# Hybrid encoder layer on one core: last gate multiplied into blocks on chip, sums held one product ahead, residuals and scale rows loaded in the middle of products

## The chip, the core and the metric

The kernel runs on one core of a Trainium2 chip. TensorE (PE) multiplies matrices, VectorE (DVE), ScalarE (ACT) and GpSimd (POOL) do elementwise work, SyncE (SP) issues most DMAs, and GpSimd issues some. The metric is device time in microseconds; the kernel before took 2562.34 us (median of three runs, 2558.35 to 2562.83).

## The reference

The layer normalises 1280 tokens of width 2048 (a prompt of 1024 and a sample of 256), projects them, runs neighbourhood attention on one half of the columns and a bidirectional mLSTM on the other, gates both, and projects the mixed rows back onto the residual:

```python
    hn = rmsnorm(x, norm_w)
    proj = jnp.einsum('btd,dp->btp', hn, w_in)
    ...
    att = (att * jax.nn.silu(na_g)).astype(x.dtype)
    ...
    h = rmsnorm(h, head_norm_w.reshape(ML_HEADS, ML_HEAD_DIM)).reshape(B, T, ML_WIDTH)
    mem = (h * jax.nn.sigmoid(ml_o.astype(f32)) * jax.nn.silu(ml_z.astype(f32))).astype(x.dtype)
    mixed = jnp.concatenate([att, mem], axis=-1)
    return x + jnp.einsum('btm,md->btd', mixed, w_out)
```

A last RMSNorm with the weights `final_norm_w` follows. Everything is in float32. The kernel reaches that precision by splitting each operand in a high and a low part (`split`: ScalarE casts the high part, VectorE subtracts it from the source for the low part) and adding three products of the parts.

## The kernel before

The end of the program is what the change touches. Tokens stand in two groups: the first 768 (`GA`) and the last 512 (`GB`). The gates of the mLSTM for the last 512 tokens are projected late, in four calls of `late_gate` (`LATE` = 0, 2, 4, 6), each for two blocks `k` of 128 mixed columns. Each call computes the gate in `z_`, loads the ungated columns of the mixed rows `mixT[k]` from DRAM into `th`, multiplies, and stores them back. The last call is for `k` = 14 and 15.

Then comes the output projection. The mixed rows are loaded by GpSimd's queue as blocks of 128 columns and 640 tokens, `mb<kh><th><kk>`: `kh` is the half of the columns, `th` the half of the tokens, `kk` one of eight blocks; `mb116` and `mb117` hold the columns 14 and 15 for the last 640 tokens. In the code the four sets are `Aa` (0,0), `Ae` (0,1), `Ad` (1,0) and `Ac` (1,1). The projection is done by a scheme of seven products in place of eight on 2 x 2 halves, once for each half `p` of the output columns, so 14 products `product(p, i, ...)`, in the order 2, 5, 1, 6, 7, 4, 3 for `p` = 0 and 5, 1, 6, 7, 4, 3, 2 for `p` = 1. Each product has eight blocks `kk`; a block is three matmuls for each of five token tiles. `operands(p, i, kk)` gives a block's two operands, which are often sums made by VectorE: of mixed blocks (`ms`, or in place in `mb01x`), of weights (`T2`, `wb`). Both operands are split (`mo` for the mixed rows, `wo` for the weights; 4 buffers each). Blocks 6 and 7 of a product (`HOLD`) are multiplied tile by tile at its end, and `reads` then adds each tile into the residual tiles `y`; `y_done` squares a finished tile (`jk`), scales it by a row of final weights (`fnb`) and stores it for `p` = 0.

Weights come on SyncE's queue in three ways: single blocks `wb` and `T` of 256 KB (six buffers `po` for `wb`), and pairs of blocks of 512 KB, which go in turn either to the two buffers that the input projection uses too (`wr_wp`) or to one tile of their own (`wp`, every third pair). Residuals are loaded into slots that the normalised inputs leave (`xslot`): for `p` = 0 on GpSimd's queue, for `p` = 1 on SyncE's.

The order of the instructions on each engine is set by a scheduler that takes from the traced program what it deems ready first; a queue is then worked off strictly in that order. `tc.issue_after(ins)` only sets such an order: what is traced inside it stands behind `ins` on the engine of `ins`, without a wait for its end.

Of the kernel before, what the change touches and what calls it, by code (L numbers as in the profile page):

```python
# [13 lines left out]
P = 128  # L14
# [31 lines left out]
def kernel(  # L46
# [23 lines left out]
    def f(ap):  # L70
        return ap.bitcast(F32)
# [91 lines left out]
    def split(hi, lo, src, scale=None):  # L163
        if scale is None:
            S.copy(hi, src)  # L165
            V.tensor_tensor(lo, src, f(hi), op=ALU.subtract)  # L166
        else:
            S.mul(hi, src, scale)
            V.scalar_tensor_tensor(lo, src, scale, f(hi), op0=ALU.mult, op1=ALU.subtract)

    def split_a(hi, lo, src):
        S.copy(hi, src)
# [520 lines left out]
        return out  # L693

    def late_gate(ch, X):
        os_ = proj_pair(OT0 + ch, X, True)
        for o_ in os_:
            S.activation(o_, o_, AF.Tanh, scale=0.5)
        for j, z_ in enumerate(proj_pair(ZT0 + ch, X, True)):
            k = 8 + ch + j  # L700
            th = po(f"lt{k}")[:, :GB]
            S.activation(th, z_, AF.Tanh, scale=0.5)
            V.scalar_tensor_tensor(z_, th, 1.0, z_, op0=ALU.add, op1=ALU.mult)
            V.scalar_tensor_tensor(z_, os_[j], 1.0, z_, op0=ALU.add, op1=ALU.mult)
            DM.dma_start(th, mixT[k][:, GA:])
            V.scalar_tensor_tensor(z_, th, w4_sb[:, k - 8 : k - 7], z_, op0=ALU.mult, op1=ALU.mult)
            DM.dma_start(mixT[k][:, GA:], z_)

    def proj_v(u, X):
        gates = u == NA_H // 2  # L710
# [764 lines left out]
        [u for us in na for u in us],  # L1475
    )
    for ch in LATE:
        late_gate(ch, X)
    att_ctx.close()

    mp = ctx.enter_context(tc.tile_pool(name="mp", bufs=1))
# [13 lines left out]
    Ad = [mix_block(1, 0, kk) for kk in range(8)]  # L1495
    Ae = [mix_block(0, 1, kk) for kk in range(8)]
    Ac = [mix_block(1, 1, kk) for kk in range(8)]
    Aa = [mix_block(0, 0, kk) for kk in range(8)]
    fnb = [xslot(28 + i, f"fnb{i}") for i in range(4)]
    T2 = {}  # L1500
    Y = {}
    ss = [mp.tile([P, 4], F32, tag=f"oss{t}", name=f"oss{t}") for t in range(2 * NT)]

    pair_of = {}

    def w_block(kh, nb, kk, name):
        raw = po(f"wb_{name}")[:, :512]
        DM.dma_start(raw, w_o[nb, :, (8 * kh + kk) * 512 : (8 * kh + kk + 1) * 512])
        return raw

    def w_pure(kh, nb, kk, name):
        k = 8 * kh + kk
        if kk % 2 == 0:
            src = w_o[nb, :, k * 512 : (k + 2) * 512]
            pair_of["n"] = pair_of.get("n", -1) + 1
            if pair_of["n"] % 3 == 2:
                pair_of["w"] = mp.tile([P, 1024], F32, tag="wr2", name=f"wp_{name}")
                DM.dma_start(pair_of["w"], src)
# [45 lines left out]
    def y_init(p, q):  # L1564
        th, nh = divmod(q, 2)
        for tt in range(NT):
            y_ = Y[p, q, tt] = xslot(q * NT + tt, f"y{p}_{q}_{tt}")
            r0 = (th * NT + tt) * P
            q_ = DM if p else G
            q_.dma_start(y_, xtok[r0 : r0 + P, (2 * p + nh) * 512 : (2 * p + nh + 1) * 512])  # L1570

    def y_done(p, q, tt):
# [9 lines left out]
    def finish(th, tt):  # L1582
# [13 lines left out]
        for i in (2, 0, 3, 1):  # L1596
# [5 lines left out]
                V.tensor_scalar(out[i], out[i], rs, None, op0=ALU.mult)  # L1602
            DM.dma_start(y[t * P : (t + 1) * P, i * 512 : (i + 1) * 512], out[i])

    HOLD = 2

    def product(p, i, bk, first, each):
        held = []
        tail = (p, i) == (1, 2)

        def mms(tt, kk, m, w, last):
# [6 lines left out]

        for kk in range(8):
            nm = f"{p}_{i}_{kk}"  # L1620
            ms, wsrc = operands(p, i, kk)
            if tail:
                m = [
                    mp.tile([P, TH], F32R, tag=f"mb{z}{z}{kk}", name=f"mo{nm}_{z}") for z in range(2)
                ]
            else:
                t = mp.tile([P, 2, TH], F32R, tag="mo", name=f"mo{nm}", bufs=4)
                m = [t[:, z] for z in range(2)]
            split(*m, ms)
            if tail and kk >= 4:  # L1630
                w = [xslot(2 * kk + 12 + z, f"wt{nm}_{z}", F32R) for z in range(2)]
            else:
                t = wb.tile([P, 2, 544], F32R, tag="wsp", name=f"wo_{nm}", bufs=4)
                w = [t[:, z, :512] for z in range(2)]
            split(*w, wsrc)
            if tail or kk >= 8 - HOLD:
                held.append((kk, m, w))
                continue
            for tt in range(NT):
                mms(tt, kk, m, w, False)  # L1640
        for tt in range(NT):
            for kk, m, w in held:
                mms(tt, kk, m, w, kk == 7)
# [4 lines left out]
    def p_banks(p, j):  # L1648
        return [bank("pr" if next(slots) == "p" else "a", f"po{p}_{j}_{i}") for i in range(NT)]

    for i in range(4):
        DM.dma_start(fnb[i], fnw[i * 512 : (i + 1) * 512].partition_broadcast(P))
    SUB = ALU.subtract
    for p in range(2):

# [124 lines left out]
```

## Time and profile before

| | |
|---|---|
| median of three runs | 2562.34 us (2558.35 to 2562.83) |
| the profiled execution | 2565.18 us, span 2563.3 us |
| TensorE busy | 2534.0 us, 99% of the span |
| VectorE, ScalarE, GpSimd busy | 77%, 52%, 24% |
| output projection, first to last matmul | 2160.00 to 2553.89 us |
| after the last matmul | last tiles added, squared, scaled and stored |
| DMA | 503.03 MB, mean 196 GB/s |

The page calls TensorE busy 99% of the span, but the ends of its matmuls are modelled, so the count of matmuls in a stretch tells more than the share. All times of the trace count from the start of the span. In its rows a name such as `wr_wp<-in_w_o_dram` is the written tile and what it is read from, with buffer numbers left out; a bracket tells how long the engine was idle just before and what ended that. `SPq` and `POOLq` are the queues on which DMAs are issued.

### The profile page before, as it was taken

Reading aid. Unit: us, or ns where it says so; the run is one execution under the profiler, and the core shown is the slowest. Engines: PE = TensorE matmul, PEld = TensorE weight load, DVE = VectorE, ACT = ScalarE, POOL = GpSimd, SP = SyncE. Lnnn points to the kernel's source line nnn. Section 1 sums busy time; section 2 is a strip of 40 time slices with the busy share of each in tenths; the row PEclk is TensorE's granted clock in tenths of the full one; section 3 lists DMA queues with packets and bytes.
Section 4 is the critical chain, followed back from the end, with each engine's and each line's share of the span. In section 5 each row is a group of like instructions: output and inputs, shape, how many; then the busy total and the mean of one; then the engine's idle time right before and its main releaser. Section 6 shows DMA issues by size and latency. Waiting matters only on the chain.

```text
span 2563.3 us, 44540 instructions
## 1 busy us (share of the span) xinstructions
PE 2534.0 (99%) x15054; PEld 2368.6 (92%) x15054; DVE 1972.6 (77%) x4029; ACT 1345.0 (52%) x3041; POOL 615.3 (24%) x909
## 2 busy tenths in 40 slices
PE   8999999999999999999999999999999999999998
PEld 8999999999999999999999999998988887788886
DVE  8769888888869798898875866765855665879695
ACT  8535545444444444465655666655745543344444
POOL 0535555444544444410001110100100104000001
PEclk9999999999999999999999999999999999999999
DMA  6546464536434342467768878877867849636237
GB/s 215 174 143 200 143 199 130 179 124 200 125 112 126 101 141 89 154 228 223 239 223 299 297 243 272 293 234 261 286 197 251 277 126 377 202 125 218 85 87 254
DMA packets 303483, 503.03 MB, mean 196 GB/s; under 512 B 48752, under 2 KB 191256, under 8 KB 303256
## 3 DMA queue, kind: packets, MB, share of 16 engines
q1 hardware_dynamic: 299096, 484.46, 58.9%
q0 software_dynamic: 4160, 15.73, 1.6%
q8 instruction: 119, 1.95, 0.3%
q14 instruction: 108, 0.88, 0.1%
HBM read 373.13 MB, written 126.95 MB: 195 GB/s over the span
## 4 chain that ended last, share of the span: by engine, by line
PE 92%; DMA 5%; DVE 2%; issue 1%; ACT 1%; SPq 0%; POOL 0%; ACTq 0%; POOLq 0%; DVEq 0%
PE pc L662 16%; PE po L1613 14%; PE pv L740 5%; PE fb L274 2%; PE A24b L274 1%; PE A12b L274 1%; PE A16b L274 1%; PE A44b L274 1%; PE A48b L274 1%; PE A52b L274 1%; PE A40b L274 1%; PE A20b L274 1%; PE A8b L274 1%; PE A50b L274 1%; PE A42b L274 1%; PE A22b L274 1%
## 5 line engine op out<-in xcount | busy, mean ns | idle before, releaser
L1613 PE MATMUL po<-wo,mo 128*128 128x512 f32 x1620 | 376.9, 393 | 3.7 <-ACT wo L165 2.8
L1613 PEld LDWEIGHTS po<-wo,mo 128*128 128x128 f32 x1620 | 303.6, 188 | 76.2 <-ACT wo L165 4.2
L166 DVE TENSOR_TENSOR ws<-wr,ws 128x512 fp32r<-128x512 f32 x152 | 104.3, 696 | 53.2 <-ACT ws L165 52.4
L165 ACT CAST ws<-wr 128x512 fp32r<-128x512 f32 x152 | 92.5, 617 | 70.1 <-PE pc L662 57.5
L165 ACT CAST mo<-mb 128x640 fp32r<-128x640 f32 x72 | 51.8, 726 | 92.5 <-PE po L1613 73.7
L116 POOL TENSOR_SCALAR rs<-rs 128x1 f32<-128x1 f32 x10 | 3.4, 341 | 351.2 <-DVE rs L1593 351.1
L166 DVE TENSOR_TENSOR mo<-mb,mo 128x640 fp32r<-128x640 f32 x72 | 59.1, 827 | 27.1 <-ACT mo L165 27.0
L1562 DVE TENSOR_TENSOR y<-y,po 128x512 f32<-128x512 f32 x90 | 58.5, 687 | 11.3 <-PE po L1613 11.0
L165 ACT CAST mo<-ms 128x640 fp32r<-128x640 f32 x40 | 28.9, 726 | 61.1 <-PE po L1613 32.1
L166 DVE TENSOR_TENSOR wsv<-wr_v,wsv 128x512 fp32r<-128x512 f32 x64 | 44.4, 700 | 14.2 <-ACT wsv L165 13.9
L165 ACT CAST wsv<-wr_v 128x512 fp32r<-128x512 f32 x64 | 39.0, 617 | 26.8 <-PE pv L740 15.5
L1576 ACT ACTIVATE jk<-y 128x512 f32<-128x512 f32 x40 | 25.2, 631 | 36.5 <-DVE y L1562 36.2
L413 DVE SCALAR_TENSOR_TENSOR pcv<-pco,cw_sb,pcv 128x516 f32<-128x516 f32 x48 | 36.7, 764 | 7.1 <-ACT pcv L407 7.0
L166 DVE TENSOR_TENSOR mo<-ms,mo 128x640 fp32r<-128x640 f32 x40 | 32.8, 823 | 7.6 <-ACT mo L165 7.6
L129 ACT ACTIVATE xq<-xq 128x1024 f32<-128x1024 f32 x20 | 21.2, 1061 | 31.7 <-DMA xq<-in_xtok_dram 29.2
L1081 POOL MEMSET mls_0v<- 128x2 f32 x4 | 0.4, 102 | 145.1 <-DVE S_dt.float L166 119.7
L274 PE MATMUL fb<-xg,fw 128*128 128x384 f32 x192 | 34.6, 334 | 0.0
L251 DVE TENSOR_TENSOR pco<-pc,rstdb 128x512 f32<-128x512 f32 x30 | 20.6, 687 | 17.8 <-PE pc L662 17.1
L274 PEld LDWEIGHTS fb<-xg,fw 128*128 128x128 f32 x192 | 33.4, 188 | 0.0
L778 DVE CUSTOM_DVE_ANT_0 nap_0st<-nap_0s,nap_0bt 128x384 f32<-128x384 f32 x32 | 17.7, 555 | 20.1 <-PE nap_0s L773 8.7
L1525 DVE TENSOR_TENSOR ms<-mb,mb 128x640 f32<-128x640 f32 x40 | 32.8, 823 | 0.0
L1492 POOL DMA_DIRECT2D mb<-mx x32 | 17.7, 554 | 58.8 <-DVE ws L166 24.8
(2655 smaller groups left out, 8512.4 us busy)
## 6 DMA issues: line engine op xcount, KB each, us to landing
wr<-in_w_in_dram SPq DMA_DIRECT2D x76, 512.0 KB, 4.7
wr_v<-in_w_in_dram SPq DMA_DIRECT2D x32, 512.0 KB, 5.0
wb<-in_w_o_dram SPq DMA_DIRECT2D x48, 256.0 KB, 3.0
xq<-in_xtok_dram SPq DMA_DIRECT2D x20, 512.0 KB, 4.2
mb<-mx POOLq DMA_DIRECT2D x32, 320.0 KB, 8.2
wr_wp<-in_w_o_dram SPq DMA_DIRECT2D x16, 512.0 KB, 4.0
vS<-vo SPq DMA_DIRECT2D x24, 256.0 KB, 5.1
nap_0bt<-in_rpb_tab_dram SPq DMA_DIRECT2D x32, 192.0 KB, 4.3
```

The source lines that it names most:

```text
L129: S.activation(raw, raw, AF.Square, accum_out=ssq[g][:, t, q : q + 1])
L165: S.copy(hi, src)
L166: V.tensor_tensor(lo, src, f(hi), op=ALU.subtract)
L251: V.tensor_tensor(o, src, rb, op=ALU.mult)
L274: PE.matmul(o, w(a_), x(b_), start=first and m == 0, stop=last and m == 2)
L413: V.scalar_tensor_tensor(dst[:, a:n], src[:, a + j - pad : n + j - pad], cw_sb[:, ct, j : j + 1], dst[:, a:n], op0=ALU.mult, op1=ALU.add,)
L662: PE.matmul(pb[j], t[j][:, wi, c : c + P], xs[xi], start=first and m == 0, stop=last and m == 2,)
L740: PE.matmul(outs[tt], xs[:, tt * P : (tt + 1) * P], t[:, wi, q * w : (q + 1) * w], start=first and m == 0 and (gates or tt % 2 == 0), stop ...
L1525: V.tensor_tensor(t, x, y_, op=op)
L1562: V.tensor_tensor(Y[p, q, tt], Y[p, q, tt], bk, op=op)
L1576: S.activation(jk, Y[p, q, tt], AF.Square, accum_out=ss[t][:, c : c + 1])
L1613: PE.matmul(bk[tt], m[xi][:, tt * P : (tt + 1) * P], w[wi], start=first and kk == 0 and j == 0, stop=last and j == 2, skip_group_check=True,)
```

## The change

There are three parts. First, the last call of `late_gate` no longer loads, multiplies and stores `mixT`: it returns its two gates, and they are multiplied into the loaded blocks `Ac[6]` and `Ac[7]` (`mb116`, `mb117`), with the same factor `w4_sb`. Second, the operands of a block are traced behind the split of the same block in the product before (`done`, filled from `now`), so that VectorE takes up a product's sums one product ahead and not sooner. Third, the residual tiles of `p` = 0 other than the first set go on SyncE's queue, and they and the scale rows are issued in the middle of products: `product` takes `loads` and the block `when` at which they are issued, behind the last `wb` load. Also every third pair of weights that goes to the tile of its own is now the first of three and no longer the last.

```diff
     def late_gate(ch, X):
+        held = []
...
             V.scalar_tensor_tensor(z_, os_[j], 1.0, z_, op0=ALU.add, op1=ALU.mult)
+            held.append(z_)
+            if ch == LATE[-1]:
+                continue
             DM.dma_start(th, mixT[k][:, GA:])
             V.scalar_tensor_tensor(z_, th, w4_sb[:, k - 8 : k - 7], z_, op0=ALU.mult, op1=ALU.mult)
             DM.dma_start(mixT[k][:, GA:], z_)
+        return held
...
     for ch in LATE:
-        late_gate(ch, X)
+        last_gates = late_gate(ch, X)
...
     Ac = [mix_block(1, 1, kk) for kk in range(8)]
+    for j, z_ in enumerate(last_gates):
+        k = LATE[-1] + j
+        t = Ac[k][:, GA - TH :]
+        V.scalar_tensor_tensor(t, t, w4_sb[:, k : k + 1], z_, op0=ALU.mult, op1=ALU.mult)
     Aa = [mix_block(0, 0, kk) for kk in range(8)]
...
     def w_block(kh, nb, kk, name):
         raw = po(f"wb_{name}")[:, :512]
-        DM.dma_start(raw, w_o[nb, :, (8 * kh + kk) * 512 : (8 * kh + kk + 1) * 512])
+        last_load["ins"] = DM.dma_start(
+            raw, w_o[nb, :, (8 * kh + kk) * 512 : (8 * kh + kk + 1) * 512]
+        ).ins
         return raw
...
-            if pair_of["n"] % 3 == 2:
+            if pair_of["n"] % 3 == 0:
...
-            q_ = DM if p else G
+            q_ = DM if p or q else G
...
+    def scales(p):
+        for i in range(4 if p == 0 else 0):
+            DM.dma_start(fnb[i], fnw[i * 512 : (i + 1) * 512].partition_broadcast(P))
+
     HOLD = 2
+    done = []
 
-    def product(p, i, bk, first, each):
+    def product(p, i, bk, first, each, loads=None, when=0):
         held = []
+        now = []
...
         for kk in range(8):
             nm = f"{p}_{i}_{kk}"
-            ms, wsrc = operands(p, i, kk)
+            if loads is not None and kk == when:
+                with tc.issue_after(last_load["ins"]) if kk else ExitStack():
+                    loads()
+            with tc.issue_after(done[kk]) if done else ExitStack():
+                ms, wsrc = operands(p, i, kk)
...
-            split(*w, wsrc)
+            now.append(split(*w, wsrc).ins)
...
+        done[:] = now
...
-    for i in range(4):
-        DM.dma_start(fnb[i], fnw[i * 512 : (i + 1) * 512].partition_broadcast(P))
...
-        y_init(p, 1)
-        y_init(p, 3)
         bk = p_banks(p, 1)
-        product(p, 5, bk, True, reads(bk, (1, ALU.add), (3, ALU.add)))
+        product(
+            p, 5, bk, True, reads(bk, (1, ALU.add), (3, ALU.add)),
+            lambda: (y_init(p, 1), y_init(p, 3)), 0 if p else 5,
+        )
...
-        product(p, 1, ch, True, reads(ch, (0, ALU.add), done=0 if p == 0 else None))
-        y_init(p, 2)
+        product(
+            p, 1, ch, True, reads(ch, (0, ALU.add), done=0 if p == 0 else None),
+            lambda: (scales(p), y_init(p, 2)), 3,
+        )
```

What the scheduler makes of it shows at three places. On SyncE's queue around the start of the output projection, before (`wr_wp_0_2_2` is the pair of weight blocks 2 and 3 of product 2, `T2` and `wb_0_5` the weights of product 5, `lt` the mixed rows for the last gate, `mx` their store):

```order
L633 DMA wr_wp_0_2_2_26553<-in_w_o_dram 128x1024
L1537 DMA T2_0_5_6_26879<-in_w_o_dram 128x512
L1537 DMA T2_0_5_7_26891<-in_w_o_dram 128x512
L1652 DMA fnb0_26476<-in_fnw_dram 128x512
L1652 DMA fnb1_26477<-in_fnw_dram 128x512
L1652 DMA fnb2_26478<-in_fnw_dram 128x512
L1652 DMA fnb3_26479<-in_fnw_dram 128x512
L633 DMA wr_wp_0_2_6_26641<-in_w_o_dram 128x1024
L705 DMA lt14_26384<-mx14_149 128x512
L1508 DMA wb_0_5_0_26715<-in_w_o_dram 128x512
L705 DMA lt15_26391<-mx15_150 128x512
L1508 DMA wb_0_5_1_26742<-in_w_o_dram 128x512
```

The same place of that queue now:

```order
L633 DMA wr_wp_0_2_4_26589<-in_w_o_dram 128x1024
L1548 DMA T2_0_5_6_26871<-in_w_o_dram 128x512
L1548 DMA T2_0_5_7_26883<-in_w_o_dram 128x512
L1529 DMA wp_0_2_6_26633<-in_w_o_dram 128x1024
L633 DMA wr_wp_0_1_0_26941<-in_w_o_dram 128x1024
L1517 DMA wb_0_5_0_26687<-in_w_o_dram 128x512
L1517 DMA wb_0_5_1_26714<-in_w_o_dram 128x512
L1517 DMA wb_0_5_2_26741<-in_w_o_dram 128x512
L1517 DMA wb_0_5_3_26768<-in_w_o_dram 128x512
L1517 DMA wb_0_5_4_26795<-in_w_o_dram 128x512
L1581 DMA y0_1_0_26822<-in_xtok_dram 128x512
L1581 DMA y0_1_1_26824<-in_xtok_dram 128x512
```

The scale rows and the loads for the last gate are gone from here, each pair of product 2's weights stands one place sooner, and ten residual tiles (the two shown and eight more) stand behind the fifth `wb`. Pair 0, which stood where pair 2 now stands (ahead of the eight `T2`), has moved to the place of the tile of its own, ahead of the last input projection's weights.

On GpSimd's queue, the end of its loads before (`y0_2_3` is a residual tile, `mb116` and `mb117` the mixed blocks of the last gate):

```order
L1570 DMA y0_2_3_27177<-in_xtok_dram 128x512
L1570 DMA y0_2_4_27179<-in_xtok_dram 128x512
L1570 DMA y0_3_0_26700<-in_xtok_dram 128x512
L1492 DMA mb116_26456<-mx14_149 128x640
L1492 DMA mb117_26458<-mx15_150 128x640
L116 TENSOR_SCALAR rs5_29151<-rs5_29151 128x1
```

And the end of its loads now:

```order
L1497 DMA mb007_26470<-mx7_142 128x640
L1581 DMA y0_0_0_26486<-in_xtok_dram 128x512
L1581 DMA y0_0_1_26488<-in_xtok_dram 128x512
L1581 DMA y0_0_2_26490<-in_xtok_dram 128x512
L1581 DMA y0_0_3_26492<-in_xtok_dram 128x512
L1581 DMA y0_0_4_26494<-in_xtok_dram 128x512
L116 TENSOR_SCALAR rs5_29147<-rs5_29147 128x1
```

Of the 20 residual loads five are left, and `mb116` and `mb117` now stand behind `mb113`, 10 loads ahead of the first residual.

On VectorE, the splits of product 1's first blocks before (`mo_0_1`, `wo_0_1`), with the first sums for product 7 (`wb_0_7`):

```order
L166 TENSOR_TENSOR wo_0_1_0_26954<-wr_wp_0_1_0_26949,wo_0_1_0_26954 128x512
L1545 TENSOR_TENSOR T2_0_5_7_26891<-wb_0_1_7_27107,T2_0_5_7_26891 128x512
L1553 TENSOR_TENSOR wb_0_7_0a_27362<-wb_0_7_0a_27362,wb_0_7_0b_27364 128x512
L166 TENSOR_TENSOR mo0_1_1_26975<-mb001_26462,mo0_1_1_26975 128x640
L166 TENSOR_TENSOR wo_0_1_1_26978<-wr_wp_0_1_0_26949,wo_0_1_1_26978 128x512
L1549 TENSOR_TENSOR mb017_26442<-mb017_26442,mb007_26474 128x640
L1553 TENSOR_TENSOR wb_0_7_1a_27390<-wb_0_7_1a_27390,wb_0_7_1b_27392 128x512
```

Where these sums stand now, among the splits of product 6 (`mo0_6`, `wo_0_6`):

```order
L166 TENSOR_TENSOR wo_0_6_0_27181<-T2_0_5_0_26689,wo_0_6_0_27181 128x512
L1564 TENSOR_TENSOR wb_0_7_0a_27358<-wb_0_7_0a_27358,wb_0_7_0b_27360 128x512
L1536 TENSOR_TENSOR ms0_7_0_27363<-mb110_26438,mb010_26422 128x640
L166 TENSOR_TENSOR mo0_6_1_27200<-mb011_26424,mo0_6_1_27200 128x640
L1573 TENSOR_TENSOR y0_0_0_26486<-y0_0_0_26486,po0_2_0_26933 128x512
L166 TENSOR_TENSOR wo_0_6_1_27203<-T2_0_5_1_26716,wo_0_6_1_27203 128x512
L1564 TENSOR_TENSOR wb_0_7_1a_27386<-wb_0_7_1a_27386,wb_0_7_1b_27388 128x512
```

The sums for product 7 have moved from product 1's splits, two products ahead, to product 6's, one ahead.

More of the change, by code (lines that the diff above doesn't have):

```diff
@@ L165, in split @@
             S.copy(hi, src)
-            V.tensor_tensor(lo, src, f(hi), op=ALU.subtract)
+            return V.tensor_tensor(lo, src, f(hi), op=ALU.subtract)
         else:
             S.mul(hi, src, scale)
-            V.scalar_tensor_tensor(lo, src, scale, f(hi), op0=ALU.mult, op1=ALU.subtract)
+            return V.scalar_tensor_tensor(lo, src, scale, f(hi), op0=ALU.mult, op1=ALU.subtract)
     def split_a(hi, lo, src):
@@ L1502 @@
     ss = [mp.tile([P, 4], F32, tag=f"oss{t}", name=f"oss{t}") for t in range(2 * NT)]
-    pair_of = {}
+    pair_of, last_load = {}, {}
     def w_block(kh, nb, kk, name):
         raw = po(f"wb_{name}")[:, :512]
-        DM.dma_start(raw, w_o[nb, :, (8 * kh + kk) * 512 : (8 * kh + kk + 1) * 512])
+        last_load["ins"] = DM.dma_start(
+            raw, w_o[nb, :, (8 * kh + kk) * 512 : (8 * kh + kk + 1) * 512]
+        ).ins
         return raw
```

## The prediction, on record before the changed kernel ran

> **What bounds the kernel now.** First the page's table of engines and its costliest group, then the stages that the change touches.
>
> ```profile
> PE 2534.0 (99%) x15054; PEld 2368.6 (92%) x15054; DVE 1972.6 (77%) x4029; ACT 1345.0 (52%) x3041; POOL 615.3 (24%) x909
> L1613 PE MATMUL po<-wo,mo 128*128 128x512 f32 x1620 | 376.9, 393 | 3.7 <-ACT wo L165 2.8
> ```
>
> TensorE is the bound, and in the output projection (L1613) it is idle for only 3.7 us. So the change can win no more than what TensorE loses there. The next view gives TensorE's matmuls in order of time: start, length, what, how many, and the wait in brackets; the last row is the end of the projection. The one after it counts the projection's matmuls in a stretch without waits.
>
> ```profile
> 2160.00 7.10 PE L1613 MATMUL po<-wo,mo 128*128 128x512 f32 x30
> 2168.93 15.68 PE L1613 MATMUL po<-wo,mo 128*128 128x512 f32 x65 [1.83 <-ACT wo L165]
> 2185.08 12.99 PE L1613 MATMUL po<-wo,mo 128*128 128x512 f32 x55 [0.47 <-DVE wo L166]
> 2199.01 1.65 PE L1613 MATMUL po<-wo,mo 128*128 128x512 f32 x6 [0.94 <-ACT wo L165]
> 2201.03 39.26 PE L1613 MATMUL po<-wo,mo 128*128 128x512 f32 x169 [0.37 <-DVE wo L166]
> ...
> 2550.95 2.94 PE L1613 MATMUL po<-wt,mo 128*128 128x512 f32 x12
> ```
>
> ```profile
> 2210.00:2530.00 320.00, 320.00 (x1385) 259.55 (x1384) 51.77 (x80) 1.00 0.48 151
> ```
>
> The projection has 14 products of 8 blocks of 15 matmuls: 1680 (1620 with `wo`, 60 with `wt`). The stretch of 320 us holds 1384 (one of the 1385 only reaches into it): 0.2312 us each, 3.47 us a block, 27.7 us a product. 1680 of them make 388.4 us, and 0.2 for the last one's longer end; the projection takes 2553.89 - 2160.00 = 393.9. So it loses 5.3 us, all before 2201: 3.61 in the four waits, the rest in starting up again after each. That is the whole prize.
>
> Why it waits: the queues. Of SyncE's queue, in order of issue (start, length, what); then ScalarE's casts of the weights, with their waits; then the DMA queues between 2116 and 2176 us.
>
> ```profile
> 2117.40 0.33 SPq L1518 DMA_DIRECT2D wp<-in_w_o_dram  x1
> 2144.86 0.33 SPq L633 DMA_DIRECT2D wr_wp<-in_w_o_dram  x1
> 2147.82 5.94 SPq L1537 DMA_DIRECT2D T<-in_w_o_dram  x6
> 2153.86 1.47 SPq L633 DMA_DIRECT2D wr_wp<-in_w_o_dram  x1
> 2155.42 0.85 SPq L1537 DMA_DIRECT2D T<-in_w_o_dram  x2
> 2159.25 4.79 SPq L1652 DMA_DIRECT2D fnb<-in_fnw_dram  x4
> 2165.76 0.33 SPq L633 DMA_DIRECT2D wr_wp<-in_w_o_dram  x1
> 2170.10 0.33 SPq L1508 DMA_DIRECT2D wb<-in_w_o_dram  x1
> ```
>
> ```profile
> 2168.26 1.14 ACT L165 CAST wo<-wr_wp 128x512 fp32r<-128x512 f32 x2 [0.40 <-DMA wr_wp<-in_w_o_dram]
> 2181.65 0.62 ACT L165 CAST wo<-wr_wp 128x512 fp32r<-128x512 f32 x1 [8.20 <-DMA wr_wp<-in_w_o_dram]
> ```
>
> ```profile
> DMA packets 7184, 22.76 MB, mean 379 GB/s; under 512 B 1119, under 2 KB 1119, under 8 KB 7180
> q0 software_dynamic: 3702, 14.13, 60.9%
> q1 hardware_dynamic: 3478, 8.58, 38.1%
> wr_wp<-in_w_o_dram SPq DMA_DIRECT2D x4, 512.0 KB, 7.1
> T<-in_w_o_dram SPq DMA_DIRECT2D x8, 256.0 KB, 10.7
> fnb<-in_fnw_dram SPq DMA_DIRECT2D x4, 256.0 KB, 15.1
> ```
>
> The DMA engines are full (60.9 + 38.1%) exactly while the first product wants its weights. The second pair of its weight blocks (issue 2153.86) is usable at 2168.2, 14.4 us later; block 2 wanted it at 2160.0 + 2 x 3.47 = 2166.9, splits included. The fourth pair (issue 2165.76) is usable at 2181.65, 15.9 us later. The scale rows stand between the two on SyncE's queue, and GpSimd's queue (mixed blocks and residuals) takes three fifths of the engines. The two waits after 2198 follow from it: `wb` for the next product is issued only at 2170.10, and VectorE does its late splits and the sums in one heap.
>
> **The change, part by part.**
>
> *Residuals and scale rows later.* GpSimd's queue in this stage:
>
> ```profile
> 2152.77 0.55 POOL L1570 DMA_DIRECT2D y<-in_xtok_dram  x1 [0.62 <-PE pc L662]
> 2174.28 0.56 POOL L1570 DMA_DIRECT2D y<-in_xtok_dram  x1 [0.56 <-issue]
> 2188.56 0.55 POOL L1492 DMA_DIRECT2D mb<-mx  x1 [13.73 <-DMA mx<-pco]
> y<-in_xtok_dram POOLq DMA_DIRECT2D x20, 256.0 KB, 7.7
> ```
>
> The 20 residual loads are issued 2152.77 to 2174.28, 1.13 us apart. 15 of them (3.9 MB) leave this queue, and 4 scale rows (1.05 MB) leave SyncE's. At 379 GB/s that is 13 us of full engines taken out of the stage. GpSimd then ends its loads near 2152.8 + 5 x 1.13 + 2 x 1.13 (the two mixed blocks that move forward) = 2160.7, landed by about 2168.4 (+ 7.7), where before it ended 2182. Cost where they go: 10 residuals now stand on SyncE's queue behind the fifth `wb` of product 5, 9 loads behind the third of product 1. In issue: 10 x 0.45 us (`T`, two in 0.85, is the nearest row; a scale row takes 1.2, 4.79 / 4) and 4 x 1.2 + 5 x 0.45 = 7.1 us. What is queued behind them is `wb` 5 of product 5, wanted at 2160.0 + 27.7 + 5 x 3.47 = 2205, and `wb` 3 of product 1, wanted in product 6, after 2243. With `wb` of product 5 issued before 2170 both are over 20 us early: I take 0, bounds 0 to 4.5.
>
> *The order of the weight pairs.* With `% 3 == 0` the first pair, not the third, sits in the tile of its own and comes with the load at 2117.40. The second pair takes the place of the load at 2144.86, the third that at 2153.86. So block 2's weights land 9 us earlier (no wait: 1.83 and its restart), block 4's at 2168.2, wanted at 2173.9. The fourth must now wait until the first is split, about 2159.3, where the first scale row was issued. By that row (15.1 to landing) it is there at 2174.4, and its doubled size costs at most 0.7 more; block 6 wants it, splits included, at 2160.0 + 6 x 3.47 - 1.3 = 2179.5. Four us early: the 0.47 goes.
>
> *The last gate.* Two loads and two stores of 256 KB of the mixed rows and their two-way trip go; the two multiplications stay, from the row before `T`'s sums to the loaded block:
>
> ```profile
> 2183.67 0.75 DVE L706 SCALAR_TENSOR_TENSOR pco<-lt,w_sb,pco 128x512 f32<-128x512 f32 x1
> 2191.84 0.55 POOL L1492 DMA_DIRECT2D mb<-mx  x1 [2.73 <-DMA mx<-pco]
> ```
>
> 2 x 0.75 us on VectorE either way, now right after the gate, where VectorE waited anyway. Blocks 6 and 7 of the mixed rows, which came last (2191.84), are then there before product 5. 1 MB less traffic. All this is cover for the same four waits, so it is not added again.
>
> *Sums held back.* VectorE may take up the sums for a block of a product only behind the split of that block in the product before. It adds no instruction. Whether VectorE still fits is read from starts in a busy stretch and from the busiest 100 us:
>
> ```profile
> 2202.22 0.70 DVE L166 TENSOR_TENSOR wo<-T,wo 128x512 fp32r<-128x512 f32 x1
> 2202.82 0.70 DVE L1538 TENSOR_TENSOR T<-T,wb 128x512 f32<-128x512 f32 x1
> 2203.43 0.83 DVE L166 TENSOR_TENSOR mo<-mb,mo 128x640 fp32r<-128x640 f32 x1
> 2204.16 0.70 DVE L1538 TENSOR_TENSOR T<-T,wb 128x512 f32<-128x512 f32 x1
> 2300.00:2400.00 100.00, 100.00 (x433) 80.92 (x432) 92.42 (x143) 49.98 (x95) 0.00 (x0) 1.00 0.60 191
> ```
>
> Busy times overlap: a 512-wide instruction takes 0.60 from start to start, a 640-wide one 0.73. The heaviest products are 7 and 4. Product 7: 16 splits 8 x 1.33 = 10.6, own sums 8 x 1.33 = 10.6, five adds of product 6, 3.0: 24.2 of 27.7 us. Product 4: 10.6, eight sums 4.8, and of product 7 ten adds and five scalings, 9.0: 24.4. Each fits even with nothing done ahead, so I cost it at nothing; the cover is these 3.3 us a product. Bounds: a gain of the two late waits (1.31, VectorE no longer does products 6's and 7's sums in the heap at 2188 to 2200) to a loss, below.
>
> *Sum.* The four waits and their restarts go, nothing is late next: -5.3 us. The profiled execution takes 2565.18 us (span 2563.3); it would take 2559.9. The median of the runs is 2.84 lower, 2562.34: 2557.0. The runs of before lie from 2558.35 to 2562.83 us, 0.17% apart; 0.2%, 5.1 us, is about what a measurement can tell from no change.
>
> A rule against the move between queues: the Trainium skill, "DMA: Bandwidth & Descriptors", section "Issuing engines are not separate DMA queues", says that transfers of SyncE, ScalarE and GpSimd share the same engines and interleave. By it, moving 15 loads from GpSimd to SyncE wins 0 by itself, and all 5.3 must come from the later place; the two queues' shares above, 99% together, agree. The section "Queues, rings and completion order" lets an engine take turns between queues packet by packet; the row agrees, with 3702 to 3478 packets, of 3.8 and 2.5 KB each.
>
> **The rivals.**
>
> *The last pair is late still.* If the engines stay full of what remains and the fourth pair is usable only at 2181.6 as before, block 6 waits 2181.6 - 2179.5 = 2.1 us, and the two waits after 2198 (1.31) stay. Then 5.3 - 3.4 = 1.9 is won: 2560.4. For it: the fourth pair depends on one tile and stands behind the eight `T`. Against it: 6.4 us earlier issue, and GpSimd's queue done 14 us earlier.
>
> *VectorE becomes the bound* (slower). Taken at full length instead of from start to start (row means 0.82 and 0.69), product 7 needs 8 x 1.51 x 2 + 5 x 0.69 = 27.6 of its 27.7 us. Before, its sums were done up to two products ahead; held back, nothing hides an overrun. It decides once VectorE's work in a product passes 27.7 us. If products 7 and 4 of both passes overrun by a tenth, 2.8 us each, that is 11.2 - 5.3 = 5.9 slower: 2568.2. Against it: the starts above, and that no wait shows even in the 100 us with VectorE at 92.42.
>
> The granted clock falls to half twice in the whole trace:
>
> ```profile
> 1635.70:1639.00 3.30, 3.30 (x18) 3.30 (x17) 3.13 (x10) 1.95 (x6) 1.77 (x6) 0.50 1.07 390
> 1734.70:1738.00 3.30, 3.30 (x16) 3.30 (x15) 2.53 (x9) 1.17 (x4) 0.00 (x0) 0.50 1.02 373
> ```
>
> Each costs about 1.7 us, outside the stages that change; one dip more or less moves a run by as much, so I widen by two on either side. The Trainium skill ("TensorE: Matmul & The Clock Gate", "What's actually happening") ties such a dip to an idle window of about 3.4 us; by it the four waits, at most 1.83, cost no clock and neither would the rival's 2.1, and the row of 320 us (1.00) agrees.
>
> **How the numbers follow.** All waits gone: 0.74, 2557.0, own range 2553.6 to 2560.4 (two dips). Last pair late: 0.14, 2560.4. VectorE the bound: 0.12, 2568.2. A wait that hangs on arriving bytes is longer in some executions than in the one profiled, and the change takes it out at whatever length, so of the 0.74 I put 0.50 beyond 5.1 us and 0.24 short of it. Faster 0.50, same 0.24 + 0.14 = 0.38, slower 0.12. Range 2553.5 to 2562.5: it leaves out the slower case and little else.
>
> **What would show it.** Matmuls of the projection from first to last in 388.6 us with no wait in the first two products; the first product's weights usable before 2176; SyncE's `wb` for product 5 issued before 2170; VectorE in the 100 us from 2300 still near 90. Wrong if TensorE waits on `wo` near block 6 of the first product, or on VectorE in products 7 and 4.

## The result, and the profile after

The changed kernel takes 2556.01 us (median of 15 runs, 2554.73 to 2559.96), the kernel before, in 15 runs beside it, 2562.22 us (2558.35 to 2565.02). The ratio is 0.9978, with a 95% interval from 0.9971 to 0.9985: faster by 0.22%. The profiled execution of after takes 2556.84 us, with a span of 2555.1 us.

First the page of after: busy time of the engines, and the projection's costliest group (the same line as L1613 before).

```profile
PE 2531.9 (99%) x15054; PEld 2367.1 (93%) x15054; DVE 1973.5 (77%) x4029; ACT 1345.0 (53%) x3041; POOL 600.7 (24%) x894
L1630 PE MATMUL po<-wo,mo 128*128 128x512 f32 x1620 | 375.5, 393 | 0.0
```

Then TensorE's matmuls in order of time (start, length, what, count; a bracket would hold a wait), the projection's first and last row, and below them the stretch that was quoted of before.

```profile
2156.85 83.40 PE L1630 MATMUL po<-wo,mo 128*128 128x512 f32 x360
...
2542.53 2.94 PE L1630 MATMUL po<-wt,mo 128*128 128x512 f32 x12
```

```profile
2210.00:2530.00 320.00, 320.00 (x1386) 259.77 (x1385) 265.48 (x409) 145.67 (x268) 9.37 (x10) 1.00 0.46 148
```

The idle time ahead of the group fell from 3.7 us to 0.0. The 360 matmuls from 2156.85 on are the first 24 blocks, three products, without a bracket, where before had four in the first two. From first to last matmul the projection takes 2545.47 - 2156.85 = 388.6 us, and took 393.9: 5.3 us less, at the same 1385 or 1386 matmuls in 320 us. The profiled executions differ by 8.3 us. Another 3.15 lie ahead of the projection (2160.00 to 2156.85; the end behind it is 0.2 longer): before had two dips of the granted clock there (stretches at half clock), about 1.7 us each, and this execution one. The rest of that is not explained here; the two kernels' orders first differ in the last stage of the input projection.

The queues of after, in the rows that answer to those of before: SyncE's issues, ScalarE's cast of the fourth pair of weights, and the DMA queues from 2116 to 2176 us.

```profile
2150.71 0.38 SPq L633 DMA_DIRECT2D wr_wp<-in_w_o_dram  x1
...
2154.74 0.33 SPq L1529 DMA_DIRECT2D wp<-in_w_o_dram  x1
...
2159.76 5.81 SPq L1517 DMA_DIRECT2D wb<-in_w_o_dram  x5
2165.86 7.74 SPq L1581 DMA_DIRECT2D y<-in_xtok_dram  x10
```

```profile
2171.59 1.14 ACT L165 CAST wo<-wp 128x512 fp32r<-128x512 f32 x2
```

```profile
DMA packets 8096, 23.78 MB, mean 396 GB/s; under 512 B 1157, under 2 KB 1157, under 8 KB 8091
...
q1 hardware_dynamic: 5131, 11.93, 52.2%
q0 software_dynamic: 2960, 11.80, 50.4%
```

The fourth pair of weights (`wp`) is issued at 2154.74 and used at 2171.59, 14.7 us into the projection and 6 us before TensorE reaches block 6 (2156.85 + 6 x 3.47 = 2177.7). The first five `wb` of product 5 go out from 2159.76, 2.9 us after the first matmul; before, the first went out after 10.1. The residuals stand behind them. But the DMA engines are as full as they were: 396 GB/s in place of 379. So full engines alone do not make TensorE wait in the projection: what changed is which loads stand ahead of the weights.

### The profile page after: what moved, and what is told of

The parts are those of the page before. It is cut to its first block, busy times and chain, and to the rows that moved or that the text cites. A ratio compares the mean times of both kernels' runs of the same rounds, so it can differ in the third digit from the quotient of the medians.

```text
span 2555.1 us, 44546 instructions
## 1 busy us (share of the span) xinstructions
PE 2531.9 (99%) x15054; PEld 2367.1 (93%) x15054; DVE 1973.5 (77%) x4029; ACT 1345.0 (53%) x3041; POOL 600.7 (24%) x894
## 3 DMA queue, kind: packets, MB, share of 16 engines
q0 software_dynamic: 2960, 11.80, 1.2%
## 4 chain that ended last, share of the span: by engine, by line
PE 83%; DMA 2%; DVE 1%; ACT 0%; issue 0%; SPq 0%; POOL 0%; ACTq 0%; POOLq 0%; DVEq 0%
PE pc L662 17%; PE po L1630 15%; PE pv L745 5%; PE A16b L274 1%; PE A48b L274 1%; PE A40b L274 1%; PE A52b L274 1%; PE A20b L274 1%; PE A44b L274 1%; PE A54b L274 1%; PE A46b L274 1%; PE A22b L274 1%; PE A18b L274 1%; PE A70b L274 1%; PE A38b L274 1%; PE A50b L274 1%
## 5 line engine op out<-in xcount | busy, mean ns | idle before, releaser
L1587 ACT ACTIVATE jk<-y 128x512 f32<-128x512 f32 x40 | 25.2, 630 | 27.9 <-DVE y L1573 27.6
L786 ACT ACTIVATE nap_0st<-nap_0st,nap_0sm 128x384 f32<-128x384 f32 x32 | 19.7, 615 | 20.7 <-DVE nap_0sm L783 20.4
```

Of the source, the lines that this page charges most:

```text
L1587: S.activation(jk, Y[p, q, tt], AF.Square, accum_out=ss[t][:, c : c + 1])
```

## The experiments

Four parts were taken alone and in combinations: the order of the weight **pairs**, the later **loads** (residuals and scale rows), the last **gate**, and the sums **held** back. The measure is the projection from first to last matmul, since the whole time also carries the clock dips and the scatter of the stages ahead of it (the first matmul came anywhere from 2153.4 to 2160.0 us, in work that the parts hardly touch). One kernel profiled twice gave 388.55 and 388.56. Each kernel was made from after by taking the other parts back; the edit shown is what it then has more than before, or less than after. Four of the sixteen combinations were not run: pairs with loads, loads with gate, loads with held, gate with held.

| parts that are in | projection, us | TensorE waits, us | that execution, us |
|---|---|---|---|
| none (before) | 393.9 | 1.83, 0.47, 0.94, 0.37 | 2565.18 |
| pairs | 396.25 | 1.33, 1.76, 0.23, 0.17 | 2564.53 |
| loads | 390.59 | 1.33 | 2557.32 |
| gate | 395.94 | 1.98, 0.88, 0.39, 0.97 | 2562.95 |
| held | 391.72 | 2.10, 0.36 | 2560.07 |
| pairs, gate | 390.63 | 0.73, 0.60 | 2557.33 |
| pairs, held | 393.48 | 1.33, 1.26, 1.39 | 2561.78 |
| loads, gate, held | 390.26 | 1.33 | 2557.34 |
| pairs, gate, held | 388.55 | none | 2553.00 |
| pairs, loads, held | 388.65 | none | 2554.39 |
| pairs, loads, gate | 390.22 | 0.97 | 2559.34 |
| all (after) | 388.6 | none | 2556.84 |

Of most kernels there is one execution, so the table is read by the projection and by the rows below, not by the last column. Before, run beside them, took 2563.34 us with the four single parts and 2558.54 us with the four that lack one part (a single run each time), and 2561.78 us (median of 15) with the rest.

**The pairs alone.** Edit of before:

```
-            if pair_of["n"] % 3 == 2:
+            if pair_of["n"] % 3 == 0:
```

> Before with one edit: the first, not the third, of three weight pairs goes to the tile of its own. Metric: output projection, start of the first matmul to end of the last, 393.9 us before, 388.6 after. By the prediction the wait at block 2 goes (1.83 us and its restart), but bytes and scale rows are still in the queues, so the weights of the next product stay late: 390.5 to 393. If the order of the pairs were all of it: 388.6 to 389. If the whole were a matter of bytes: 393.9, with the wait at block 2 moved to a later block.

TensorE's matmuls from the start of the projection, and the granted clock behind the second wait (the last three columns of a stretch are clock, DMA share and GB/s):

```profile
2156.86 27.95 PE L1624 MATMUL po<-wo,mo 128*128 128x512 f32 x120
2186.14 0.72 PE L1624 MATMUL po<-wo,mo 128*128 128x512 f32 x2 [1.33 <-ACT wo L165]
2188.62 9.53 PE L1624 MATMUL po<-wo,mo 128*128 128x512 f32 x28 [1.76 <-DVE wo L166]
```

```profile
2188.70:2195.20 6.50, 6.50 (x16) 5.08 (x17) 1.93 (x3) 0.58 (x1) 0.00 (x0) 0.54 0.61 211
```

The first product now runs its 120 matmuls without a wait. So the pair order does what the prediction says of it. But the time comes back as two waits at block 8, the first of product 5: after 120 matmuls for the high part of its weights, and two matmuls later for the low part. (Block 9, which the expectations name too, does not wait: the 28 matmuls behind carry TensorE to block 10.) TensorE reaches block 8 sooner, and VectorE's first sum for it (`T` and `wb`) starts at 2184.60, as late as before (2184.93). The two waits close together were followed by 6.8 us at half clock (16 matmuls in 6.5 us, where 28 fit); half of 6.8 us is 3.4, and without the dip the projection would take about 392.8. So the measured 396.25 lies outside the range expected, by the dip.

**The loads alone.**

```
-            q_ = DM if p else G
+            q_ = DM if p or q else G
...
-    for i in range(4):
-        DM.dma_start(fnb[i], fnw[i * 512 : (i + 1) * 512].partition_broadcast(P))
...
-        y_init(p, 1)
-        y_init(p, 3)
...
+            lambda: (y_init(p, 1), y_init(p, 3)), 0 if p else 5,
...
-        y_init(p, 2)
...
+            lambda: (scales(p), y_init(p, 2)), 3,
```

> Before with one edit: residuals and scale rows loaded in the middle of products. By the prediction the fourth pair and the next product's weights come in time, but the second pair is issued where it was, ahead of which GpSimd's loads still fill the engines: the first wait (1.83 us and its restart, 2.3) stays, the rest goes: 390.5 to 391.5. If bytes were all of it: 388.6. If these loads were hidden anyway: 393.9.

```profile
2155.93 7.10 PE L1624 MATMUL po<-wo,mo 128*128 128x512 f32 x30
2164.36 363.14 PE L1624 MATMUL po<-wo,mo 128*128 128x512 f32 x1568 [1.33 <-ACT wo L165]
```

After 30 matmuls, at block 2, TensorE still waits for the second pair; everything behind it is gone. The later loads alone win 3.3 us of 5.3, as expected, but not the wait at block 2.

**The gate alone.**

```
+            if ch == LATE[-1]:
+                continue
...
+    for j, z_ in enumerate(last_gates):
+        k = LATE[-1] + j
+        t = Ac[k][:, GA - TH :]
+        V.scalar_tensor_tensor(t, t, w4_sb[:, k : k + 1], z_, op0=ALU.mult, op1=ALU.mult)
```

> Before with one edit: the last gate multiplied into the loaded blocks. By the prediction this is cover and frees nothing that TensorE waits for: 393 to 394.5. If the round trip of the gated rows were what delays the second product: the two waits after 2198 (1.31 us) go as well, 392 to 392.6.

```profile
2155.83 7.10 PE L1630 MATMUL po<-wo,mo 128*128 128x512 f32 x30
2164.91 57.40 PE L1630 MATMUL po<-wo,mo 128*128 128x512 f32 x240 [1.98 <-ACT wo L165]
```

```profile
2165.90:2169.20 3.30, 3.30 (x9) 2.59 (x9) 1.49 (x3) 0.52 (x2) 1.64 (x3) 0.51 1.03 385
```

No gain, but 2 us more than before, above the range expected: block 2 waits as before, and 3.4 us at half clock follow, which cost about 1.7. The two waits after 2198 do go, but others come, for VectorE: 0.88 us in the third product, and 0.39 and 0.97 at the start of product 3.

**The held sums alone.**

```
-            ms, wsrc = operands(p, i, kk)
+            with tc.issue_after(done[kk]) if done else ExitStack():
+                ms, wsrc = operands(p, i, kk)
...
+        done[:] = now
```

> Before with one edit: sums held one product ahead. By the prediction it costs and wins nothing but, at best, the two waits at the end of VectorE's heap: 392.5 to 394. By the rival (VectorE becomes the bound) 396 or more, with waits on VectorE in products 7 and 4.

```profile
2157.07 7.09 PE L1624 MATMUL po<-wo,mo 128*128 128x512 f32 x30
2166.26 14.97 PE L1624 MATMUL po<-wo,mo 128*128 128x512 f32 x63 [2.10 <-ACT wo L165]
2181.58 63.60 PE L1624 MATMUL po<-wo,mo 128*128 128x512 f32 x274 [0.36 <-DVE mo L166]
```

The two waits after 2198 are gone though `wb` was as late as before: the first goes out 10.3 us after the first matmul, before 10.1. VectorE no longer does its heap of sums there. 2.2 us are won, more than expected, by an edit that was costed at nothing.

**All but the pairs.** Edit of after:

```
-            if pair_of["n"] % 3 == 0:
+            if pair_of["n"] % 3 == 2:
```

> After, with the third of three weight pairs in the tile of its own again. If the second pair's issue (behind most of the T2 loads) makes the first wait, the wait at block 2 is back as with the loads alone (1.33 us), and nothing else: projection 390.0 to 391.0. If the later loads make up for the order: 388.6.

```profile
2164.10 362.59 PE L1630 MATMUL po<-wo,mo 128*128 128x512 f32 x1567 [1.33 <-ACT wo L165]
```

The wait at block 2 is back (the first matmul is at 2155.68, and 30 ran before it), and nothing else: 1.65 us. In all five executions without the pair order TensorE waits at block 2, for 1.33 to 2.10 us, and in none of the nine with it.

**All but the loads.** After, with the edit of the loads above taken back:

> After, with residuals and scale rows loaded where they were before. If GpSimd's bytes keep the next product's weights late, waits stand at the start of the second product (block 8 and 9), as with the pairs alone: 390 to 392.5 without a dip of the clock. If the order of the pairs, the gate and the held sums suffice together: 388.6 to 389.

TensorE's matmuls, then SyncE's issues:

```profile
2153.35 369.31 PE L1630 MATMUL po<-wo,mo 128*128 128x512 f32 x1597
```

```profile
2153.49 6.03 SPq L1618 DMA_DIRECT2D fnb<-in_fnw_dram  x4
...
2163.71 10.38 SPq L1517 DMA_DIRECT2D wb<-in_w_o_dram  x6
```

No wait in 1597 matmuls, with the four scale rows back ahead of `wb` and all 20 residuals back on GpSimd's queue. `wb` of product 5 goes out 10.4 us after the first matmul, 7.5 later than in after, and that is early enough. It is the second alternative of what was expected.

**All but the gate.** After, with the edit of the gate taken back:

> After, with the last gated rows loaded, multiplied and stored as before. If this part is cover alone: 388.6 to 389, no wait. If the blocks 6 and 7 that then come last delay VectorE's sums for product 5: a wait at its blocks 6 and 7, 389.5 to 391.

```profile
2154.80 369.40 PE L1624 MATMUL po<-wo,mo 128*128 128x512 f32 x1597
```

Nothing is lost either. So loads and gate could each be left out alone; the run with pairs and held sums, below, asks whether both can.

**All but the held sums.** Edit of after:

```
-        done[:] = now
```

> After, with VectorE free to take up sums as early as it can. The held sums alone won 2.2 us over before, so if they act by thinning VectorE's heap at the start of product 5, a small wait of 0.3 to 1.5 us is back there: 388.9 to 390.5. If the heap came from the late weights alone, which are in time here: 388.6.

TensorE's rows, then VectorE's in order of time up to the wait:

```profile
2157.75 169.65 PE L1630 MATMUL po<-wo,mo 128*128 128x512 f32 x732
2328.36 200.59 PE L1630 MATMUL po<-wo,mo 128*128 128x512 f32 x866 [0.97 <-DVE y L1573]
```

```profile
2315.20 0.69 DVE L1549 TENSOR_TENSOR T<-T,wb 128x512 f32<-128x512 f32 x1 [2.06 <-DMA wb<-in_w_o_dram]
...
2321.00 1.36 DVE L1549 TENSOR_TENSOR T<-T,wb 128x512 f32<-128x512 f32 x2 [1.89 <-DMA wb<-in_w_o_dram]
...
2327.62 0.68 DVE L1573 TENSOR_TENSOR y<-y,po 128x512 f32<-128x512 f32 x1
```

TensorE waits at the start of product 3 of the first pass (732 matmuls are six products of 120, and four of the five token tiles of the next one's first block) for the adds of product 4 into `y`, which free its banks. VectorE had stood idle for 2.06 and 1.89 us just before, for weights of sums two products ahead, and the adds stand behind these in its order. Taken up early, a sum does not only come early: it makes everything behind it wait for a load that nothing needs yet. The size was expected (0.3 to 1.5 us), the place was not: at the start of product 5 nothing waits.

**Two parts without the loads.** The edits of pairs and gate in before; then those of pairs and held sums:

> Before with the pair order and the gate on chip, sums as early as before, residuals and scale rows where they were. If the gate's loads and stores on SyncE's queue are what kept the next product's weights late in the run with the pairs alone, the waits at blocks 8 and 9 go and what remains is a wait of VectorE's sums at the later products: 389 to 390.5 us. If the held sums are needed for block 8: waits of 0.5 to 2 us there, 390 to 392 or, with a dip of the clock, 393.5.

```profile
2155.50 28.41 PE L1630 MATMUL po<-wo,mo 128*128 128x512 f32 x122
2184.65 141.28 PE L1630 MATMUL po<-wo,mo 128*128 128x512 f32 x610 [0.73 <-DVE wo L166]
2326.54 200.58 PE L1630 MATMUL po<-wo,mo 128*128 128x512 f32 x866 [0.60 <-DVE y L1573]
```

With the gate on chip, 0.73 us of the waits at block 8 and 0.60 at product 3 are left, where the sums are taken up early: 390.63 us, a wait at block 8 as the second alternative has it.

> Before with the pair order and the held sums, the gate's rows loaded, multiplied and stored as before, residuals and scale rows where they were. If the gate's transfers ahead of the wb loads are the cause: waits at blocks 8 and 9 as with the pairs alone, 390.5 to 392.5, up to 396 with a dip. If VectorE's heap is: none or one small, 388.6 to 389.5.

TensorE, SyncE and, of VectorE, what stands up to the first sum for product 5 (`pco` is the gate's multiplication):

```profile
2157.10 27.92 PE L1624 MATMUL po<-wo,mo 128*128 128x512 f32 x120
2186.36 0.72 PE L1624 MATMUL po<-wo,mo 128*128 128x512 f32 x2 [1.33 <-ACT wo L165]
2188.34 6.73 PE L1624 MATMUL po<-wo,mo 128*128 128x512 f32 x28 [1.26 <-DVE wo L166]
```

```profile
2156.97 6.06 SPq L1612 DMA_DIRECT2D fnb<-in_fnw_dram  x4
...
2167.04 2.22 SPq L707 DMA_DIRECT2D lt<-mx  x2
2171.58 2.19 SPq L1511 DMA_DIRECT2D wb<-in_w_o_dram  x2
...
2183.66 0.33 SPq L709 DMA_DIRECT2D mx<-pco  x1
2184.04 0.42 SPq L1511 DMA_DIRECT2D wb<-in_w_o_dram  x1
```

```profile
2182.28 0.69 DVE L1567 TENSOR_TENSOR y<-y,po 128x512 f32<-128x512 f32 x1 [0.70 <-PE po L1624]
2182.89 0.75 DVE L708 SCALAR_TENSOR_TENSOR pco<-lt,w_sb,pco 128x512 f32<-128x512 f32 x1
2183.66 0.69 DVE L1567 TENSOR_TENSOR y<-y,po 128x512 f32<-128x512 f32 x1
2184.27 0.75 DVE L708 SCALAR_TENSOR_TENSOR pco<-lt,w_sb,pco 128x512 f32<-128x512 f32 x1
2184.93 0.68 DVE L1543 TENSOR_TENSOR T<-T,wb 128x512 f32<-128x512 f32 x1
```

And the same place of VectorE in the run without the later loads alone, where nothing waits:

```profile
2178.54 0.69 DVE L1573 TENSOR_TENSOR y<-y,po 128x512 f32<-128x512 f32 x1 [0.22 <-PE po L1630]
2179.14 0.68 DVE L1549 TENSOR_TENSOR T<-T,wb 128x512 f32<-128x512 f32 x1
```

Here is the rest of the mechanism. With scale rows and gate both in place, SyncE issues the scale rows, a pair, the two loads of the gate, and only then the first two `wb`, 14.5 us after the first matmul; without the gate's transfers it is 10.4. Yet the first `wb` takes 10.7 us to land in the one and 14.8 in the other, so it is there 25.2 us after the first matmul in both. What differs is VectorE's own order. In both its third add of product 2's tiles starts 25.2 us after the first matmul. Without the gate's multiplications the first sum for product 5 follows at 25.8; with them, two multiplications and an add come in between, none with a wait for a load, and it starts at 27.8, when its block is already wanted (27.7). That delay of 2.0 us stands right ahead of the two waits at block 8 (1.33 and 1.26). The third `wb` stands behind the gate's store, which waits for VectorE's multiplication, and goes out at 2184.04; its sum, at 2193.21, stands directly behind a split that waited 2.20 us for ScalarE, so how much of the third wait (1.39) is due to the late issue is not shown. With the later loads in (all but the gate) the multiplications are done by 2174.6 and the first sum follows at once, 19.7 us after the first matmul.

So take away either the scale rows and residuals or the gate's loads, multiplications and stores, and the 4.9 us between 393.48 and 388.6 are won; the second of them adds nothing. The 393.48 has no dip and lies above both ranges expected.

**VectorE loaded further.** One more 512-wide add per block, 8 x 0.60 = 4.8 us a product; its result is used by nothing.

```
             now.append(split(*w, wsrc).ins)
+            xx = mp.tile([P, 512], F32, tag="xx", name=f"xx{nm}", bufs=1)
+            V.tensor_tensor(xx, wsrc, wsrc, op=ALU.add)
```

> After, with one more addition of 128x512 per block on VectorE (a block's weights to themselves, written to a tile that nothing reads): 8 x 0.60 = 4.8 us a product, output unchanged. By the prediction's slack (products 7 and 4 at 24.2 and 24.4 of 27.7 us) these overrun by 1.3 to 1.5 us each and the others take part of it up: projection 389 to 395, with waits on VectorE near products 7 and 4. If VectorE had no slack: 14 x 4.8 = 67 us more. If it had 5 us in each product: 388.6.

Time 2580.7 us, projection 404.83: 16.2 us more than after, and more than the 389 to 395 expected. TensorE first, then ScalarE's cast for which it waited longest, both at product 3 of the first pass; then VectorE's busy time (the figure with x43, behind TensorE and its weight loads) in the same product of after, without the added work.

```profile
2157.68 180.23 PE L1630 MATMUL po<-wo,mo 128*128 128x512 f32 x780
...
2352.56 161.00 PE L1630 MATMUL po<-wo,mo 128*128 128x512 f32 x690 [5.71 <-ACT wo L165]
```

```profile
2351.89 1.14 ACT L165 CAST wo<-wr_wp 128x512 fp32r<-128x512 f32 x2 [1.76 <-DMA wr_wp<-in_w_o_dram]
```

```profile
2323.00:2351.00 28.00, 28.00 (x123) 22.69 (x122) 27.14 (x43) 13.04 (x25) 0.00 (x0) 1.00 0.67 225
```

In after, VectorE is busy for 27.14 of the 28.00 us of this product: no 3.3 us are free there. With 4.8 us more TensorE waits in this product: 0.69 and 0.81 us for VectorE's splits, then 5.71 us at block 6, for a pair of weights that is still loading when its cast is due. That pair goes out at 2346.54, after SyncE waited 1.6 us for the added addition itself, which reads a block's weights once more and so holds their buffer longer; in after the same pair goes out at 2319.39. The wait is accompanied by 6.8 us at half clock, from 2348.9. So the run shows that product 3 has no 4.8 us free, but not how much of the 16.2 is VectorE's time alone. The second pass has waits in the same product again, smaller ones (1.61, 1.30, 1.17, 1.33, 0.55).

**All but the loads, timed.** The kernel without the later loads was run in rounds beside before:

> After without the later residuals and scale rows, timed. If these loads are worth nothing beside the other three parts: the same ratio to before as after's, 0.9978 within 0.001. If the margin that they give (the weights of product 5 landing about 12 us before they are wanted, against 1 to 2 us without) is needed in some executions: 0.9985 to 0.9995.

2555.72 us (median of 11, 2553.70 to 2559.06) against 2561.78 (15, 2559.35 to 2565.82): ratio 0.9978, interval 0.9969 to 0.9987, the same as for the whole change. No version beats after by what can be measured; this one does as well with fewer edits.

## Why the prediction was right, and where its reasons were not

**The sum: right.** It put the prize at 5.3 us, all in four waits before 2201, and let all of it go: 5.3 measured in the projection, no wait left. 2557.0 was forecast, 2556.01 is the median. Against the shared runs of before, 2562.22, the median moved by 6.2; the 0.9 beyond 5.3 is within the interval (1.8 us on either side) and is not explained further.

That the whole sum came out is in part luck: no single part the forecast counts on clears all four waits, and without the held sums, which it costed at nothing, 1.6 us of the 5.3 would have been missing (390.22).

**"Residuals and scale rows later": sufficient for most, and not necessary.** The step saw "13 us of full engines taken out of the stage". The runs contradict its reasoning twice. The loads alone leave the first wait standing (1.33 us at block 2). And with all of these loads back where they were, the other three parts still remove every wait, at 396 GB/s, as full as before. What counted was the place of a few loads in SyncE's own order (the pairs) and of a few instructions in VectorE's (the sums). Nor do "the two waits after 2198" follow from the late `wb` alone: the held sums remove them with `wb` issued as late as before. The cost of 0 where the loads go was right, though the ten residual issues took 7.74 us, above the bound of 4.5. So was the remark that `wb` of product 5 would be issued before 2170 (2159.76). One reading was off: GpSimd did not end its loads by 2182 before, since `mb117` is issued only at 2191.84; the sum does not use it.

**"The order of the weight pairs": right,** and more than the step claimed: it is the only part without which the wait at block 2 stays. Alone it wins nothing, since TensorE then stands at block 8 for sums that are as late as before, which the step did not ask.

**"All this is cover for the same four waits": right with the later loads, wrong without them.** With the loads in, the gate is worth nothing (388.65 against 388.6). Without them it is worth 4.9 beside pairs and held sums: its two multiplications stand in VectorE's order ahead of the first sum for product 5, and its loads and stores in SyncE's order among the `wb`. Gate and loads are two ways to the same thing, so neither cost nor gain of either can be read from a single removal.

**"Sums held back", at nothing: the term that was mis-sized.** It is worth 2.2 us alone, 2.1 on top of pairs and gate, and 1.6 in the whole change. Alone, these are the two late waits of the bound (1.31) and their restarts. In the whole change it is another wait, at product 3 (0.97 us and its restart), which before does not show. In the seven executions with held sums and no added work TensorE never waits there; of the six without, four do (0.17 to 0.97 us in one wait), and why before and the loads alone do not is open.

**"These 3.3 us a product": wrong.** Products 7 and 4 were costed, product 3 was not. In after it carries its splits, 10.6, eight sums of mixed blocks, 8 x 0.73 = 5.9, eight sums of weights for the next product, 4.8, and ten adds and scalings for product 4, 6.0: 27.3 of 27.7 us. The row of 27.14 busy of 28.00 agrees. It fits, so the forecast held, but with 0.4 us to spare, not 3.3.

**The rivals.** "The last pair is late still" fell: the pair was issued at 2154.74, 4.5 us sooner than the step had it (3.15 of these because the projection itself began sooner), and was cast at 2171.59, 6 us before TensorE reached block 6. "VectorE becomes the bound" fell with the opposite sign: holding back the sums helped VectorE. Yet its point of decision, 27.7 us of work in a product, lay nearer than the forecast thought.

**"The four waits, at most 1.83, cost no clock": true of these four, not of waits of that length.** A wait of 1.98 us was followed by 3.4 us at half clock, and two of 1.33 and 1.76 by 6.8 us. Others, of 2.10 and 1.33 us, were followed by none:

```profile
2157.00:2181.00 24.00, 21.90 (x94) 17.22 (x93) 12.78 (x20) 6.66 (x11) 7.67 (x14) 1.00 1.04 390
```

That row is of the kernel with the held sums alone, around its wait of 2.10 us; its granted clock is 1.00. The two dips of before follow waits too: TensorE stood idle for 2.54 us up to 1634.38 and for 1.86 us up to 1733.96, and half clock began at 1635.66 and at 1734.65. The Trainium skill ("TensorE: Matmul & The Clock Gate", "What's actually happening") has the array fall to half clock after an idle window of about 3.4 us that runs freely. The lengths of the dips, one and two such windows, agree; that they can follow waits of 2 us and less goes beyond what the forecast took from it.

The traces show what tells the cases apart. In each execution the changes of the granted clock lie whole multiples of 3.41 us apart (28 of them between the two dips of before, 95.57 us). Cut into cells by that grid, the cell ahead of a dip held 2.14 and 1.86 us of idle TensorE in before, 1.98 with the gate alone, and 2.35 with the pairs alone (1.33 and the first 1.02 of the next wait). The wait of 2.10 us was cut by a boundary into 1.1 and 1.0, and before's 1.83 into 1.0 and 0.8. In the fourteen executions traced, start and end left aside and with matmul ends as the profile models them, every cell with at least 1.82 us idle was followed by half clock. Of the cells with 1.2 to 1.8 us two were, and one dip, of after, came behind a wait of 1.19 us. So it is the idle time within one cell, and not the length of a wait, that fits nearly all cases; no run was made to test it.

**By its own marks:** 388.6 us with no wait in the first two products, as stated; the first product's weights usable by 2171.6 (before 2176). VectorE in the 100 us from 2300 was to stay near 90 and fell to 84.49, a mark that was missed without harm:

```profile
2300.00:2400.00 100.00, 100.00 (x434) 81.18 (x433) 84.49 (x129) 49.17 (x89) 0.00 (x0) 1.00 0.55 177
```

## What to carry to other kernels

When a load is late on full DMA engines, look first at what stands ahead of it on its own queue: one place sooner for each pair removed here the first wait, which taking 13 us of traffic away did not. When a sum is late, see whether its load was: here the load had landed in time, and two multiplications stood ahead of the sum in VectorE's order. A removed wait only counts when the next load in line is also early enough, so try parts in pairs: a part that wins nothing alone (the pair order) can be the one without which a wait stays, and two parts (loads and gate) can stand for each other. On an engine that works strictly in order, doing work early is not free: it can put a wait for a far load ahead of work that is due now, so cost every product's load, the last one too, before calling slack.

## What the hardware showed that was not expected

- Two queues on full engines did not get equal packets: from 2116 to 2176 us before had 3702 and 3478 packets, after 2960 and 5131, at about 100% of the engines both times. How long each queue had nothing waiting was not counted, so this does not show how an engine chooses between two queues with work.
- Half clock of 3.4 and 6.8 us came behind waits of 1.98 us and of 1.33 and 1.76 us, and none behind 2.10 us. Where half clock follows, a short wait costs 1.7 to 3.4 us beyond its length. Whether it follows went, in nearly all cases, with the idle time inside one cell of a grid of 3.41 us: from 1.82 us on it always did.
